# Keys and queries turned to feature layout by VectorE in 32x32 blocks, into tiles that already exist

## The chip, the cores and the metric

The kernel runs on one core of a Trainium2 chip. TensorE (PE in the profile) multiplies, VectorE (DVE) and ScalarE (ACT) work elementwise, GpSimd (POOL) does small things beside them, and SyncE (SP) issues nearly all transfers. Each engine works through its own list of instructions in order and waits at semaphores for the others. The metric is the time on the device in microseconds (us): the median of three runs before is 2010.44 us (2010.2 to 2012.16).

## What is computed

One layer of a streaming encoder, for 256 frames of a new stream (prompt) and 8 running streams with 16 frames each (sample). Together these are 384 tokens, three tiles of 128. What matters here, cut from the reference:

```
h   = rmsnorm(x);  proj = h @ w_in        # columns: GLU in | q | k | v | forget | gate A | gate B
q   = rmsnorm(q, q_norm_g);  k = rmsnorm(k, k_norm_g)      # 8 heads of 128
prompt:  softmax(q k^T / sqrt(128) + bias, causal) v
sample:  the same over 128 old keys and values of each stream, and its own new frames
u   = glu_a * sigmoid(glu_b);  depthwise conv over 31 frames, layernorm, swish, pointwise
x   = x + (sigmoid(gA) * conv_branch + sigmoid(gB) * attention) @ w_out
x   = x + gated FFN with a short convolution
```

Keys, values and forget logarithms of the new frames are outputs too.

## The kernel before

**Products.** Each float32 weight is split in two float32r parts, `hi` (a rounded copy, ScalarE, L145) and `lo` (the rest, VectorE, L146), and the activations likewise, so each product is three matmuls: hi·hi, hi·lo, lo·hi. `gemm` (L219 on) works on *blocks* of two k-tiles of weights (256 rows by 512 columns; a job of 16 k-steps takes 8 blocks). Three tags have three buffers each: `raw` (the block as loaded), `hi` and `lo`. A block's `hi` can be made only when TensorE has done with the block three places earlier, since that one's buffer is taken. So in steady state a `hi` starts when TensorE ends block n-3, and TensorE needs the split block after two more blocks.

**Order.** TensorE's list stands in program order (`manual_schedule` for that engine, L289). The lists of VectorE, ScalarE and SyncE are made by a scheduler from priorities; the splits (`ahead`, L197) and the evacuations have a raised priority. Once built, each list is fixed.

**The stages around the change.** The projection jobs run in this order: v (three jobs), k (two), q (two), GLU (four jobs of kind "A", where the weights are stationary and the 384 tokens stream by, L237 to L239), then the gates. k and q lie in `kt` and `qt`, tokens on the partitions. After the k jobs VectorE norms the keys (L517, L518) and after the q jobs the queries (L526), in the background of the next jobs.

**Attention** is done by steps hung on the k-steps of the four GLU jobs: after each k-step `tick` runs one step of `attention()` and one of `conv()`. A dictionary says at which tick a step of which head comes: `ATT_FIRST + 6 * head + offset`. The steps of one head are: `head_past_keys` (old keys turned by VectorE, L569), `head_operands` (three transposes of the queries and three of the new keys on TensorE into PSUM, L581 and L585, brought back by ScalarE as `qT` with a scale, L582, and by VectorE as `kT`, L586; then VectorE copies the sample queries into a zero-padded tile `qz`, L587), `head_scores` (products L593 to L601, the last eight of them with `qz`; then the softmax), `head_probs`, `head_out` and `head_last` (which write the head's rows of `attT`). `misc` PSUM tiles (three) serve all of these.

**Block transposes.** `blocks` (L253) already exists for the later stages: sixteen VectorE instructions at L257 turn three token tiles by 512 columns into feature layout. Each takes one group of 32 partitions, 12 blocks of 32x32.

Of the kernel before, what the change touches and what calls it, by code (L numbers as in the profile page):

```python
# [8 lines left out]
F32 = mybir.dt.float32  # L9
F32R = mybir.dt.float32r  # L10
AF = mybir.ActivationFunctionType
# [4 lines left out]
P = 128  # L16
DM = 2048
NT = 384
NTT = 3
H = 8  # L20
# [5 lines left out]

O_A, O_B, O_Q, O_K, O_V, O_GA, O_GB = 0, 1024, 2048, 3072, 4096, 5128, 7176

ATT_FIRST = 5
CONV_FIRST, CONV_LAG = 24, 17  # L30
LN_LAG = 18
SQ_LAG = 1
# [8 lines left out]
def hybrid_step(  # L41
# [9 lines left out]
    nc = tc.nc  # L51

    def pool(name, side="left", bufs=1, space=None):
        kw = dict(name=name, bufs=bufs, reuse_waits="tile")
        if space is not None:
            kw["space"] = space
        else:
            kw["side"] = side
        cm = tc.tile_pool(**kw)
        p = cm.__enter__()  # L60
        return p, lambda: cm.__exit__(None, None, None)
# [11 lines left out]
    def misc_tile():  # L73
        return misc.tile([P, 512], F32, tag="misc", name="misc")
# [4 lines left out]
    mm = nc.tensor.matmul  # L79
    tr = nc.tensor.transpose  # L80
# [26 lines left out]
    ident = cp.tile([P, P], F32, name="ident")  # L107
# [145 lines left out]
    def blocks(rows, put):  # L253
        src = rows.rearrange("p t (m b j) -> p b m t j", m=4, b=4)
        for b in range(4):
            for a in range(4):
                nc.vector.transpose(put(a, slice(32 * b, 32 * b + 32)), src[32 * a:32 * a + 32, b])  # L257

    def by_feature(dst):
        return lambda a, js: dst[js].rearrange("p m (t a i) -> p m t a i", t=NTT, a=4)[:, :, :, a]  # L260
# [75 lines left out]
    attT = p_t.tile([P, H, NT], F32, tag="T", name="attT")  # L336
# [3 lines left out]
    kt = p_qkv.tile([P, NTT, 1024], F32, name="kt")  # L340
    qt = p_qkv.tile([P, NTT, 1024], F32, name="qt")
# [36 lines left out]
    qgs = cp.tile([P, 1], F32, name="qgs")  # L378
# [136 lines left out]
    for t in range(NTT):  # L515
        k3 = kt[:, t, :].rearrange("p (h d) -> p h d", h=H)
        tt(k3, k3, rk[:, t, :].unsqueeze(2).to_broadcast([P, H, P]), op=ALU.mult)  # L517
        tt(k3, k3, kg[:].unsqueeze(1).to_broadcast([P, H, P]), op=ALU.mult)  # L518
    nc.sync.dma_start(prompt_k[0, 0].rearrange("(t p) h d -> p t (h d)", p=P), kt[:, 0:2, :])
    nc.sync.dma_start(sample_k[0].rearrange("b t h d -> (b t) (h d)"), kt[:, 2, :])  # L520

# [2 lines left out]
    for t in range(NTT):  # L524
        q3 = qt[:, t, :].rearrange("p (h d) -> p h d", h=H)
        tt(q3, q3, rq[:, t, :].unsqueeze(2).to_broadcast([P, H, P]), op=ALU.mult)  # L526


    p_att, close_att = pool("att", side="right")
    qz = [p_att.tile([P, 4, 2, 48], F32, name=f"qz{i}") for i in range(2)]  # L530
# [4 lines left out]
    def by_stream(ap):  # L535
        return ap.rearrange("p (g r t) -> p g r t", g=4, r=2)

    def padded(t_, b):
        r = b % 2
        return t_[:, b // 2].rearrange("p r x -> p (r x)")[:, 32 * r:32 * r + 32]  # L540
# [3 lines left out]
    def load_k(h):  # L544
        kc = kcs[h] = p_att.tile([P, 8 * P], F32, tag="kc", bufs=2, name="kc")
        for a in range(4):
            q = slice(32 * a, 32 * a + 32)
            nc.sync.dma_start(kc[q, :].rearrange("k (b j d) -> k b j d", b=8, j=4),
                              cache_k[0, :, :, h, q].rearrange("b (j k) d -> k b j d", j=4))

    def load_v(h):
        vc = p_att.tile([P, 8, P], F32, tag="vc", bufs=2, name="vc")
        nc.sync.dma_start(vc[:], cache_v[0, :, :, h, :].rearrange("b p d -> p b d"))
        bs = p_att.tile([P, 5 * P], F32, tag="bs", bufs=2, name="bs")
        nc.sync.dma_start(bs[:, 0:P], c_dr[h, 0:P].partition_broadcast(P))
        nc.sync.dma_start(bs[:, P:3 * P], c_dr[h, 0:2 * P].partition_broadcast(P))
        nc.sync.dma_start(bs[:, 4 * P:5 * P], c_dr[h, 2 * P:3 * P].partition_broadcast(P))
        nc.sync.dma_start(bs[:, 3 * P:4 * P], d_dr[:].rearrange("(b h) k -> b h k", h=H)[:, h:h + 1, :]
                          .to_broadcast([8, 16, P]))
        bc = bs[:, :4 * P].rearrange("p (a x) -> p a x", x=2 * P)[:, :, :P]  # L560
        nc.gpsimd.tensor_tensor(bc, bc, mk[:, 0:1, :].to_broadcast([P, 2, P]), op=ALU.add)
        nc.gpsimd.tensor_tensor(bs[:, 4 * P:], bs[:, 4 * P:], mk[:, 1, :], op=ALU.add)
        vbs[h] = vc, bs
# [3 lines left out]
    def head_past_keys(d):  # L567
        kTs = p_att.tile([P, 8, P], F32, tag="kTs", bufs=1, name="kTs")
        nc.vector.transpose(kTs[:].rearrange("p b k -> p (b k)"), kcs[d["h"]][:])  # L569
        d["kTs"] = kTs  # L570
        if d["h"] + 1 < H:
            load_k(d["h"] + 1)

    def head_operands(d):
        hs = d["hs"]
        d["vc"], d["bs"] = vbs[d["h"]]
        qT = p_att.tile([P, NT], F32, tag="qT", bufs=2, name="qT")
        kT = p_att.tile([P, NT], F32, tag="kT", bufs=2, name="kT")
        ps = misc_tile()
        for t in range(NTT):  # L580
            tr(ps[:, t * P:(t + 1) * P], qt[:, t, hs], ident[:])  # L581
        nc.scalar.activation(qT[:], ps[:, :NT], AF.Identity, scale=qgs[:])  # L582
        ps = misc_tile()
        for t in range(NTT):
            tr(ps[:, t * P:(t + 1) * P], kt[:, t, hs], ident[:])  # L585
        nc.vector.tensor_copy(kT[:], ps[:, :NT])  # L586
        nc.vector.tensor_copy(qz[d["h"] % 2][:, :, :, 0:16], by_stream(qT[:, 2 * P:]))  # L587
        d["qT"], d["kT"] = qT, kT

    def head_scores(d):  # L590
        qT, kT, kTs, bs, qzh = d["qT"], d["kT"], d["kTs"], d["bs"], qz[d["h"] % 2]
        s0 = misc_tile()
        mm(s0[:, :P], qT[:, 0:P], kT[:, 0:P], start=True, stop=True)  # L593
        s1 = misc_tile()
        mm(s1[:, :2 * P], qT[:, P:2 * P], kT[:, 0:2 * P], start=True, stop=True)  # L595
        s2_ = misc_tile()
        mm(s2_[:, P:2 * P], qT[:, 2 * P:], kT[:, 2 * P:], start=True, stop=True)
        for r in range(2):
            for g in range(4):
                b = 2 * g + r  # L600
                mm(s2_[32 * g:32 * g + 32, :P], padded(qzh, b), kTs[:, b, :], start=r == 0, stop=r == 1)  # L601
        pr = p_att.tile([P, 5 * P], F32, tag="pr", bufs=2, name="pr")
        mx = p_att.tile([P, 9], F32, tag="mx", bufs=2, name="mx")
        segs = [(s0, 0, 1), (s1, 1, 2), (s2_, 3, 2)]
        for i, (sp_, o, n) in enumerate(segs):
            v = pr[:, o * P:(o + n) * P]
            nc.vector.tensor_tensor_reduce(out=v, in0=sp_[:, :n * P], in1=bs[:, o * P:(o + n) * P], scale=1.0,
                                           scalar=-3.0e38, op0=ALU.add, op1=ALU.max, accum_out=mx[:, i:i + 1])
            ts(mx[:, 3 + i:4 + i], mx[:, i:i + 1], -1.0, None, op0=ALU.mult)
            nc.scalar.activation(v, v, AF.Exp, bias=mx[:, 3 + i:4 + i], accum_out=mx[:, 6 + i:7 + i])  # L610
            nc.vector.reciprocal(mx[:, i:i + 1], mx[:, 6 + i:7 + i])
            nc.scalar.activation(v, v, AF.Identity, scale=mx[:, i:i + 1])
        d["pr"] = pr
# [35 lines left out]
    def attention():  # L649
        at = {}  # L650
        for d in heads:
            for off, step in ((0, head_past_keys), (2, head_operands), (4, head_scores), (9, head_probs),
                              (11, head_out), (13, head_last)):
                at[ATT_FIRST + 6 * d["h"] + off] = step, d
        for t in range(max(at) + 1):
            if t in at:
                step, d = at[t]
                step(d)
                if step is head_out and d["h"] + 2 < H:
                    load_v(d["h"] + 2)  # L660
            yield
# [78 lines left out]
    load_v(0)  # L740
    load_v(1)
    att_steps = attention()
    gemm([job("A", 16, ha, glu_evac(g)) for g in range(4)], [att_steps, conv_steps])
    drain(att_steps)
# [175 lines left out]
    for u, i0 in enumerate(range(0, 11, 3)):  # L920
        n = min(3, 11 - i0)
# [141 lines left out]
```

## Time and profile before

| | |
|---|---|
| median of three runs | 2010.44 us |
| the profiled execution | 2010.56 us |
| its span, first to last instruction | 2008.6 us |
| TensorE busy | 1998.5 us, 99% |
| VectorE busy | 1242.1 us, 62% |
| ScalarE busy | 741.6 us, 37% |

The profiled execution is the one the rows are from; 2.0 us of its time lie outside the span. Busy shares are means over the whole span. A timeline row gives the start, the duration, the engine, the line and operation, what it writes and reads, how many instructions were merged, and in brackets how long the engine was idle before and for whom it waited. Matmuls overlap: the duration of one is longer than the distance to the next, so their pace is read from the starts.

### The profile page before, as it was taken

Reading aid. Unit: us, or ns where it says so; the run is one execution under the profiler, and the core shown is the slowest. Engines: PE = TensorE matmul, PEld = TensorE weight load, DVE = VectorE, ACT = ScalarE, POOL = GpSimd, SP = SyncE. Lnnn points to the kernel's source line nnn. Section 1 sums busy time; section 2 is a strip of 40 time slices with the busy share of each in tenths; the row PEclk is TensorE's granted clock in tenths of the full one; section 3 lists DMA queues with packets and bytes.
Section 4 is the critical chain, followed back from the end, with each engine's and each line's share of the span. In section 5 each row is a group of like instructions: output and inputs, shape, how many; then the busy total and the mean of one; then the engine's idle time right before and its main releaser. Section 6 shows DMA issues by size and latency. Waiting matters only on the chain.

```text
span 2008.6 us, 24550 instructions
## 1 busy us (share of the span) xinstructions
PE 1998.5 (99%) x9494; PEld 1686.6 (84%) x9494; DVE 1242.1 (62%) x1806; ACT 741.6 (37%) x1083; POOL 84.6 (4%) x214
## 2 busy tenths in 40 slices
PE   9999999999999999999999999999999999999999
PEld 8988999988888888888888888888888888888887
DVE  4434478888762645576767684367673376638663
ACT  5434454433333523334333432233332233323321
POOL 1000011100000000000000010000000000000000
PEclk9999999999999999999999999999999999999999
DMA  6566466344433353334343434434443434343443
GB/s 185 171 175 176 138 158 170 121 135 131 140 126 126 131 183 120 134 121 132 121 137 126 137 117 136 133 124 125 133 137 126 127 126 136 127 126 126 137 155 107
DMA packets 200574, 275.99 MB, mean 137 GB/s; under 512 B 45022, under 2 KB 88049, under 8 KB 200449
## 3 DMA queue, kind: packets, MB, share of 16 engines
q1 hardware_dynamic: 200137, 273.85, 43.5%
q8 instruction: 74, 1.21, 0.2%
q0 software_dynamic: 288, 0.57, 0.1%
q14 instruction: 43, 0.35, 0.1%
q10 hardware_dynamic: 32, 0.01, 0.0%
HBM read 266.98 MB, written 7.86 MB: 137 GB/s over the span
## 4 chain that ended last, share of the span: by engine, by line
PE 98%; DVE 1%; DMA 1%; ACT 0%; issue 0%; SPq 0%; ACTq 0%
PE acc L242 29%; PE acc L244 29%; PE acc L243 29%; PE acc L237 2%; PE acc L239 2%; PE acc L238 2%; DMA raw<-in_w_in_dram 1%; DVE uT L257 0%; DVE lo L146 0%; PE misc L845 0%; PE misc L634 0%; PE misc L601 0%; PE misc L283 0%; PE misc L620 0%; PE misc L595 0%
## 5 line engine op out<-in xcount | busy, mean ns | idle before, releaser
L146 DVE TENSOR_TENSOR lo<-raw,hi 128x1024 fp32r<-128x1024 f32 (+2 forms) x481 | 579.0, 1204 | 624.0 <-ACT hi L145 621.5
L145 ACT CAST hi<-raw 128x1024 fp32r<-128x1024 f32 (+2 forms) x481 | 496.0, 1032 | 1016.5 <-PE acc L244 900.3
L242 PE MATMUL acc<-hi,xg 128*128 128x512 f32 x1056 | 412.3, 390 | 0.0
L244 PE MATMUL acc<-hi,xg 128*128 128x512 f32 x1056 | 411.0, 389 | 0.0
L243 PE MATMUL acc<-lo,xg 128*128 128x512 f32 x1056 | 410.8, 389 | 0.0
L242 PE MATMUL acc<-hi,hT 128*128 128x512 f32 (+1 forms) x704 | 267.6, 380 | 2.0 <-ACT hT L286 2.0
L244 PE MATMUL acc<-hi,hT 128*128 128x512 f32 (+1 forms) x704 | 265.4, 377 | 0.4 <-DVE hT L287 0.4
L243 PE MATMUL acc<-lo,hT 128*128 128x512 f32 (+1 forms) x704 | 265.1, 377 | 0.0
L242 PEld LDWEIGHTS acc<-hi,xg 128*128 128x128 f32 x1056 | 198.2, 188 | 42.1
L244 PEld LDWEIGHTS acc<-hi,xg 128*128 128x128 f32 x1056 | 198.2, 188 | 41.3
L243 PEld LDWEIGHTS acc<-lo,xg 128*128 128x128 f32 x1056 | 198.3, 188 | 40.8
L242 PE MATMUL acc<-hi,act 128*128 128x512 f32 x528 | 205.5, 389 | 0.5 <-DVE y L1008 0.5
L243 PE MATMUL acc<-lo,act 128*128 128x512 f32 x528 | 205.4, 389 | 0.0
L244 PE MATMUL acc<-hi,act 128*128 128x512 f32 x528 | 205.4, 389 | 0.0
L720 DVE SCALAR_TENSOR_TENSOR ut<-ext,cw,ut 128x384 f32<-128x384 f32 x240 | 151.9, 633 | 6.2
L242 PEld LDWEIGHTS acc<-hi,hT 128*128 128x128 f32 x704 | 132.4, 188 | 24.6 <-ACT hT L286 2.3
L244 PEld LDWEIGHTS acc<-hi,hT 128*128 128x128 f32 x704 | 132.4, 188 | 23.1 <-DVE hT L287 0.7
L243 PEld LDWEIGHTS acc<-lo,hT 128*128 128x128 f32 x704 | 132.5, 188 | 22.2
L257 DVE STREAM_TRANSPOSE extf<-tok 32x384 f32<-32x384 f32 x176 | 100.3, 570 | 30.9 <-ACT tok L944 28.2
L257 DVE STREAM_TRANSPOSE uT<-tok 32x384 f32<-32x384 f32 x176 | 100.3, 570 | 29.7 <-ACT tok L944 26.9
L242 PEld LDWEIGHTS acc<-hi,act 128*128 128x128 f32 x528 | 99.1, 188 | 21.3 <-DVE y L1008 0.9
L244 PEld LDWEIGHTS acc<-hi,act 128*128 128x128 f32 x528 | 99.1, 188 | 20.7
(287 smaller groups left out, 2068.4 us busy)
## 6 DMA issues: line engine op xcount, KB each, us to landing
raw<-in_w_up_dram SPq DMA_DIRECT2D x176, 512.0 KB, 3.4
raw<-in_w_in_dram SPq DMA_DIRECT2D x96, 512.0 KB, 3.3
raw<-in_w_down_dram SPq DMA_DIRECT2D x88, 512.0 KB, 3.4
raw<-in_w_in_dram SPq DMA_DIRECT2D x64, 256.0 KB, 2.9
raw<-in_w_out_dram SPq DMA_DIRECT2D x32, 512.0 KB, 3.4
raw<-in_w_att_out_dram SPq DMA_DIRECT2D x16, 512.0 KB, 3.5
raw<-in_conv_pw_out_dram SPq DMA_DIRECT2D x16, 512.0 KB, 4.4
raw<-in_w_in_dram SPq DMA_DIRECT2D x23, 344.0 KB, 3.3
```

The costliest lines, as they stand in the source:

```text
L145: nc.scalar.copy(hi[:, k, :o], raw[:, k, :o])
L146: tt(lo[:, k, :o], raw[:, k, :o], f(hi[:, k, :o]), op=ALU.subtract)
L237: mm(o, hi[:, kk, s], ah, start=st, stop=False)
L238: mm(o, hi[:, kk, s], al, start=False, stop=False)
L239: mm(o, lo[:, kk, s], ah, start=False, stop=sp)
L242: mm(o, ah[:, s], hi[:, kk, :n], start=st, stop=False)
L243: mm(o, ah[:, s], lo[:, kk, :n], start=False, stop=False)
L244: mm(o, al[:, s], hi[:, kk, :n], start=False, stop=sp)
L257: nc.vector.transpose(put(a, slice(32 * b, 32 * b + 32)), src[32 * a:32 * a + 32, b])
L720: stt(o, v, wc, o, op0=ALU.mult, op1=ALU.add)
```

## The change

After the keys are normed, `blocks` turns them on VectorE, 32 instructions for the eight heads, into `attT`: the tile in which the attention output is put later, head by head, after that head's keys have been read. After the queries are normed, 32 more turn these into `kt`, whose token-layout keys are no longer needed; ScalarE scales them there in place, one instruction per head (L533). The per-head tiles `qT` and `kT`, the six TensorE transposes per head and the two instructions that brought them back are gone. `head_past_keys` is called by `head_operands`, at the same tick; `ATT_FIRST` goes from 5 to 8, with the other offsets kept, so scores and all later steps of a head come three ticks later (tick 12 instead of 9 for the first head).

```diff
-ATT_FIRST = 5
+ATT_FIRST = 8
...
         tt(k3, k3, kg[:].unsqueeze(1).to_broadcast([P, H, P]), op=ALU.mult)
+    for n in range(2):
+        blocks(kt[:, :, 512 * n:512 * (n + 1)], by_feature(attT[:, 4 * n:4 * n + 4]))
...
         tt(q3, q3, rq[:, t, :].unsqueeze(2).to_broadcast([P, H, P]), op=ALU.mult)
+    qT = kt[:].rearrange("p t n -> p (t n)").rearrange("p (h x) -> p h x", h=H)
+    for n in range(2):
+        blocks(qt[:, :, 512 * n:512 * (n + 1)], by_feature(qT[:, 4 * n:4 * n + 4]))
+        for h in range(4 * n, 4 * n + 4):
+            nc.scalar.activation(qT[:, h], qT[:, h], AF.Identity, scale=qgs[:])
...
     def head_operands(d):
-        hs = d["hs"]
+        head_past_keys(d)
         d["vc"], d["bs"] = vbs[d["h"]]
-        qT = p_att.tile([P, NT], F32, tag="qT", bufs=2, name="qT")
-        kT = p_att.tile([P, NT], F32, tag="kT", bufs=2, name="kT")
-        ps = misc_tile()
-        for t in range(NTT):
-            tr(ps[:, t * P:(t + 1) * P], qt[:, t, hs], ident[:])
-        nc.scalar.activation(qT[:], ps[:, :NT], AF.Identity, scale=qgs[:])
-        ps = misc_tile()
-        for t in range(NTT):
-            tr(ps[:, t * P:(t + 1) * P], kt[:, t, hs], ident[:])
-        nc.vector.tensor_copy(kT[:], ps[:, :NT])
-        nc.vector.tensor_copy(qz[d["h"] % 2][:, :, :, 0:16], by_stream(qT[:, 2 * P:]))
-        d["qT"], d["kT"] = qT, kT
+        nc.vector.tensor_copy(qz[d["h"] % 2][:, :, :, 0:16], by_stream(qT[:, d["h"], 2 * P:]))
...
-            for off, step in ((0, head_past_keys), (2, head_operands), (4, head_scores), (9, head_probs),
+            for off, step in ((0, head_operands), (4, head_scores), (9, head_probs),
```

The scheduler lays the new instructions among the others, so the diff does not say where they stand. The first place is VectorE's list during the two q jobs, from the end of the norm of the keys. Before, it holds four `lo` of weight blocks, the evacuation of the first q job (L424) and the next `lo`; these blocks are the last two of the first q job and the first three of the second:

```order
L146 TENSOR_TENSOR lo_1559<-raw_1556,hi_1558 128x1024
L146 TENSOR_TENSOR lo_1583<-raw_1580,hi_1582 128x1024
L146 TENSOR_TENSOR lo_1607<-raw_1604,hi_1606 128x1024
L146 TENSOR_TENSOR lo_1631<-raw_1628,hi_1630 128x1024
L424 TENSOR_SCALAR qt_159<-acc_1458,rs1_145 128x512
L146 TENSOR_TENSOR lo_1685<-raw_1682,hi_1684 128x1024
```

The same place of the changed kernel, with the same five blocks under new numbers (1591, 1615, 1639, 1663, 1717):

```order
L257 STREAM_TRANSPOSE attT_150<-kt_158 32x12x32
L146 TENSOR_TENSOR lo_1591<-raw_1588,hi_1590 128x1024
L257 STREAM_TRANSPOSE attT_150<-kt_158 32x12x32 x6
L146 TENSOR_TENSOR lo_1615<-raw_1612,hi_1614 128x1024
L257 STREAM_TRANSPOSE attT_150<-kt_158 32x12x32 x6
L146 TENSOR_TENSOR lo_1639<-raw_1636,hi_1638 128x1024
L257 STREAM_TRANSPOSE attT_150<-kt_158 32x12x32 x7
L146 TENSOR_TENSOR lo_1663<-raw_1660,hi_1662 128x1024
L257 STREAM_TRANSPOSE attT_150<-kt_158 32x12x32 x2
L424 TENSOR_SCALAR qt_159<-acc_1490,rs1_145 128x512
L257 STREAM_TRANSPOSE attT_150<-kt_158 32x12x32 x9
L146 TENSOR_TENSOR lo_1717<-raw_1714,hi_1716 128x1024
```

Thirty-one transposes of keys now stand ahead of the third block's `lo` of the second q job, and 22 of them ahead of the evacuation L424.

The second place is VectorE's list at the start of the GLU jobs, from the last instruction of the norm of the queries to the first head's scores. Before, `lo` of GLU blocks 5 and 6 (counted from 0), the copy of the turned keys, `qz` of the first head and the first step of its softmax:

```order
L526 TENSOR_TENSOR qt_159<-qt_159,rq1r_1905 128x1024
L146 TENSOR_TENSOR lo_2059<-raw_2055,hi_2058 128x1024
L586 COPY kT_2087<-misc_2093 128x384
L146 TENSOR_TENSOR lo_2103<-raw_2099,hi_2102 128x1024
L587 COPY qz0_1918<-qT_2086 128x8x16
L607 ISA pr_2144,mx_2145<-misc_2130,bs_1935 128x128
```

The changed kernel there; the four `lo` are those of GLU blocks 5, 6, 7 and 8:

```order
L528 TENSOR_TENSOR qt_159<-qt_159,rq1r_1937 128x1024
L257 STREAM_TRANSPOSE kt_158<-qt_159 32x12x32 x3
L146 TENSOR_TENSOR lo_2124<-raw_2120,hi_2123 128x1024
L257 STREAM_TRANSPOSE kt_158<-qt_159 32x12x32 x10
L146 TENSOR_TENSOR lo_2155<-raw_2151,hi_2154 128x1024
L257 STREAM_TRANSPOSE kt_158<-qt_159 32x12x32 x19
L146 TENSOR_TENSOR lo_2194<-raw_2190,hi_2193 128x1024
L146 TENSOR_TENSOR lo_2225<-raw_2221,hi_2224 128x1024
L584 COPY qz0_1990<-kt_158 128x8x16
L603 ISA pr_2254,mx_2255<-misc_2240,bs_2007 128x128
```

All 32 transposes of queries, and the `lo` of four blocks, now stand between the norm of the queries and `qz` of the first head.

The third place is TensorE's list where the first head's scores come, in the changed kernel: the end of the first k-step of GLU block 6, the scores, and the second k-step's first matmul:

```order
L239 MATMUL acc_2026<-hT3_88,lo_2155 128x384
L589 MATMUL misc_2240<-attT_150,kt_158 128x128
L591 MATMUL misc_2242<-attT_150,kt_158 128x256
L593 MATMUL misc_2244<-attT_150,kt_158 128x128
L597 MATMUL misc_2244<-kTs_2170,qz0_1990 32x128 x8
L237 MATMUL acc_2023<-hT3_88,hi_2154 128x384
```

The eight products with `qz0_1990` stand ahead of the rest of block 6; before, the scores stood after the tenth k-step, at the end of block 4 (lo_2021), and now after the thirteenth.

## Rows read from the trace of the kernel before

**Rows 1.** The page: busy time of the engines, and the chain by engine.

```profile
PE 1998.5 (99%) x9494; PEld 1686.6 (84%) x9494; DVE 1242.1 (62%) x1806; ACT 741.6 (37%) x1083; POOL 84.6 (4%) x214
...
PE 98%; DVE 1%; DMA 1%; ACT 0%; issue 0%; SPq 0%; ACTq 0%
```

**Rows 2.** Waits of TensorE, longest first: for whom, us, times, longest.

```profile
PE misc L306 <- POOL ident masks.py:199: 2.5, 1, 2.5
...
PE misc L706 <- DVE pz L624: 0.3, 1, 0.3
```

**Rows 3.** TensorE's timeline, first head: its transposes, the matmul after, its scores.

```profile
233.64 0.49 PE L581 MATMUL misc<-ident,qt 128*128 128x128 f32 x3
...
234.47 0.33 PE L238 MATMUL acc<-hT,hi 128*128 128x384 f32 x1
...
238.48 0.38 PE L593 MATMUL misc<-kT,qT 128*128 128x128 f32 x2
...
239.45 0.64 PE L601 MATMUL misc<-kTs,qz 128*32 128x128 f32 x16
```

**Rows 4.** Groups by line and shape: count, busy us, mean ns of one.

```profile
L257 DVE STREAM_TRANSPOSE uT<-tok 32x384 f32<-32x384 f32 x176 | 100.3, 570 | 29.7 <-ACT tok L944 26.9
...
L569 DVE STREAM_TRANSPOSE kTs<-kc 128x1024 f32<-128x1024 f32 x8 | 9.9, 1239 | 0.0
...
L582 ACT ACTIVATE qT<-misc,qgs 128x384 f32<-128x384 f32 x8 | 4.6, 576 | 3.9 <-PE misc L581 3.9
...
L587 DVE COPY qz<-qT 128x128 f32<-128x128 f32 x8 | 2.3, 289 | 0.0
```

**Rows 5.** VectorE's timeline in a later stage: block transposes with a `lo` between.

```profile
1717.47 3.49 DVE L257 STREAM_TRANSPOSE uT<-tok 32x384 f32<-32x384 f32 x6
1720.99 1.23 DVE L146 TENSOR_TENSOR lo<-raw,hi 128x1024 fp32r<-128x1024 f32 x1
1722.25 1.16 DVE L257 STREAM_TRANSPOSE uT<-tok 32x384 f32<-32x384 f32 x2
```

**Rows 6.** VectorE's timeline in the q jobs.

```profile
168.18 1.22 DVE L518 TENSOR_TENSOR kt<-kt,kg 128x1024 f32<-128x1024 f32 x1
...
183.85 0.75 DVE L424 TENSOR_SCALAR qt<-acc,rs 128x512 f32<-128x512 f32 x1 [1.10 <-PE acc L244]
```

**Rows 7.** ScalarE's timeline in the q jobs.

```profile
185.08 0.29 ACT L431 ACTIVATE jk<-qt 128x128 f32<-128x128 f32 x1
...
186.82 1.04 ACT L145 CAST hi<-raw 128x1024 fp32r<-128x1024 f32 x1
```

**Rows 8.** TensorE's timeline: second q job, its third block, first GLU job.

```profile
184.33 0.39 PE L242 MATMUL acc<-hi,hT 128*128 128x512 f32 x1
...
192.72 0.39 PE L243 MATMUL acc<-lo,hT 128*128 128x512 f32 x1
...
216.97 0.33 PE L237 MATMUL acc<-hT,hi 128*128 128x384 f32 x1
```

**Rows 9.** VectorE's timeline at the start of the GLU jobs.

```profile
228.40 1.22 DVE L526 TENSOR_TENSOR qt<-qt,rq1r 128x1024 f32<-128x1024 f32 x1
```

**Rows 10.** TensorE's timeline near the start of the program.

```profile
7.92 0.49 PE L244 MATMUL acc<-hi,hT 128*128 128x344 f32 x1
8.20 0.49 PE L242 MATMUL acc<-hi,hT 128*128 128x344 f32 x1
...
16.35 0.43 PE L242 MATMUL acc<-hi,hT 128*128 128x344 f32 x1 [2.03 <-ACT hT L286]
...
17.56 0.32 PE L242 MATMUL acc<-hi,hT 128*128 128x344 f32 x1
17.72 0.32 PE L243 MATMUL acc<-lo,hT 128*128 128x344 f32 x1
```

**Rows 11.** Windows: PE, PEld, DVE, ACT, POOL busy us, then granted clock.

```profile
300.00:350.00 50.00, 49.73 (x381) 47.18 (x380) 43.57 (x103) 25.74 (x53) 5.87 (x9) 1.00 0.72 171
350.00:395.00 45.00, 45.00 (x303) 42.80 (x302) 37.96 (x67) 21.44 (x37) 6.54 (x10) 1.00 0.37 116
```

More of the change, by code (lines that the diff above doesn't have):

```diff
@@ L574, in head_operands @@
     def head_operands(d):
-        hs = d["hs"]
+        head_past_keys(d)
         d["vc"], d["bs"] = vbs[d["h"]]
-        qT = p_att.tile([P, NT], F32, tag="qT", bufs=2, name="qT")
-        kT = p_att.tile([P, NT], F32, tag="kT", bufs=2, name="kT")
-        ps = misc_tile()
-        for t in range(NTT):
-            tr(ps[:, t * P:(t + 1) * P], qt[:, t, hs], ident[:])
-        nc.scalar.activation(qT[:], ps[:, :NT], AF.Identity, scale=qgs[:])
-        ps = misc_tile()
-        for t in range(NTT):
-            tr(ps[:, t * P:(t + 1) * P], kt[:, t, hs], ident[:])
-        nc.vector.tensor_copy(kT[:], ps[:, :NT])
-        nc.vector.tensor_copy(qz[d["h"] % 2][:, :, :, 0:16], by_stream(qT[:, 2 * P:]))
-        d["qT"], d["kT"] = qT, kT
+        nc.vector.tensor_copy(qz[d["h"] % 2][:, :, :, 0:16], by_stream(qT[:, d["h"], 2 * P:]))
     def head_scores(d):
-        qT, kT, kTs, bs, qzh = d["qT"], d["kT"], d["kTs"], d["bs"], qz[d["h"] % 2]
+        qh, kh, kTs, bs, qzh = qT[:, d["h"]], attT[:, d["h"]], d["kTs"], d["bs"], qz[d["h"] % 2]
         s0 = misc_tile()
-        mm(s0[:, :P], qT[:, 0:P], kT[:, 0:P], start=True, stop=True)
+        mm(s0[:, :P], qh[:, 0:P], kh[:, 0:P], start=True, stop=True)
         s1 = misc_tile()
-        mm(s1[:, :2 * P], qT[:, P:2 * P], kT[:, 0:2 * P], start=True, stop=True)
+        mm(s1[:, :2 * P], qh[:, P:2 * P], kh[:, 0:2 * P], start=True, stop=True)
         s2_ = misc_tile()
-        mm(s2_[:, P:2 * P], qT[:, 2 * P:], kT[:, 2 * P:], start=True, stop=True)
+        mm(s2_[:, P:2 * P], qh[:, 2 * P:], kh[:, 2 * P:], start=True, stop=True)
         for r in range(2):
```

## The prediction

> **What bounds the kernel now.** I read the page's busy times and its chain first. TensorE is busy for 99% of the span and makes up 98% of the chain that ended last [rows 1]: a microsecond of TensorE's list that goes is a microsecond won, and one that TensorE waits is one lost. Its waits come next: five groups, of which the longest is 2.5 us before its very first matmul, and the shortest, 0.3 us, the only one in the stages of the change [rows 2]. So each `lo` and each attention operand is there in time today, and the question is which of them will be late. For that I read the timelines of TensorE, VectorE and ScalarE from the norm of the keys to the first head's scores [rows 3, 6 to 9]. The attention and convolution stage itself has little air on VectorE: busy 43.57 of 50 and 37.96 of 45 us, with TensorE busy throughout [rows 11].
>
> **What goes: 5.3 us of TensorE.** Without the six transposes of a head, L237 would start where L581 does, at 233.64, and L238 0.17 us later (the distance of two such matmuls); L238 stands at 234.47 [rows 3]. That is 0.66 us per head and 5.3 us for eight. All of it is on the chain, and TensorE's list gets nothing in return. The copies back to SBUF go too, but ScalarE scales eight times as before (0.576 us each [rows 4]), and neither engine is the bound.
>
> **What comes: 64 block transposes on VectorE.** The same shape, 32x384, took 570 ns [rows 4], and six of them, up to the next instruction, 3.52 us: 0.585 us each; a `lo` among them takes 1.26 us to the next [rows 5]. Reading from `kt` or `qt` instead of `tok` changes only a stride. The other bound for the pace is the transpose of old keys, 1024 columns in 1239 ns [rows 4], which is 0.465 us for 384 columns. I take 0.585, the row with the same access pattern. 64 of them are 37.4 us, and they are hidden only as long as no `lo` and no operand behind them in VectorE's list is late. Twice one is.
>
> [...]
>
> **First wait: the keys, in the second q job.** The norm of the keys ends at 168.18 + 1.22 = 169.40 [rows 6]. From there VectorE's new list is 22 transposes and four `lo` up to the evacuation L424: 22 x 0.585 + 4 x 1.26 = 17.9, so L424 starts at 187.3 instead of 183.85 and ends at 188.05 with its 0.75 us [rows 6]. The four blocks are in time: each `lo` comes at most 7 transposes after the one before, 5.4 us with itself, and the last, done at 186.2, is wanted one block (4.08 us, [rows 8]) after 184.33, at 188.4. But two things now hang on the late evacuation. ScalarE's squares of that tile (first at 185.08) wait for it, and behind them in ScalarE's list stands the `hi` of the second job's third block, 1.74 us after that first square [rows 7]: it ends at 188.1 + 1.74 + 1.05 = 190.9, harmless. On VectorE nine more transposes stand ahead of that block's `lo`: 188.05 + 9 x 0.585 + 1.23 = 194.5. TensorE wants it at 192.72 [rows 8]. So it waits 1.9 us (with 0.1 for the handover). With the quicker pace, 0.105 us less for each of 31, there is no wait at all.
>
> **Second wait: the queries, at the first head's scores.** All later times shift by the first wait alike, so I leave it out here. The norm of the queries ends at 228.40 + 1.22 = 229.62 [rows 9]. Behind it: 32 transposes, 18.7 us; the `lo` of blocks 5 and 6 among them, 2.5; the `lo` of blocks 7 and 8 behind them, 2.4; then `qz`, some 0.25 [rows 4, 5]. That is 253.5. None of these four `lo` has to wait for its own `hi`: the latest, block 8's, may start when TensorE ends block 5, at 216.97 + 12 x 2.085 = 242.0, and stands on ScalarE behind four scalings, which can start after the sixteenth transpose (241.6) and take 2.3 us, so it ends at about 245.
>
> When does TensorE come for `qz`? A k-step is 2.085 us: ten of them and one head's transposes lie between 216.97 and 238.48 [rows 3, 8]. The scores now come after 13, at 244.07; their first three products take 0.97 us (238.48 to 239.45 [rows 3]), and at 245.05 the eight products with `qz` stop TensorE until 253.5. That is 8.5 us. The three ticks of later start give 6.25 us, and without them the wait would be longer by as much. Queued behind it is everything TensorE has, above all the rest of GLU block 6; block 7's `lo` (252.1) and block 8's (253.3) would have made TensorE wait too, but less. Behind `qz` on VectorE the first head's softmax starts late but has five ticks, 10 us, till its probabilities are wanted. Quicker pace: 32 x 0.105 less, 5.1 us.
>
> **Third term: TensorE's pace after standing still.** [...] At the start of the program, after 2.5 us without work, 344-column matmuls stood 0.28 us apart at 8 us, where they stand 0.16 apart at 17.6; but 2.03 us of waiting at 14 to 16.35 changed nothing [rows 10]. So the price of 8.5 us of standing still has these ends (a gain is excluded, the clock being at its upper level): nothing, as after the 2.03 us, or the start's, about half of the 6 us from the first matmul at 2.5 to past 8.2, some 3.0 us. A wait four times as long as the harmless one is nearer to the start; I take 2.0. The first wait, 1.9 us, is like the harmless one: nothing.
>
> [...]
>
> **Sum.** -5.3 + 1.9 + 8.5 + 2.0 = +7.1 us on the profiled execution's 2010.56 us, that is 2017.7; the median of the runs stands 0.1 us lower, so 2017.5 us, 0.35% slower. Transfers bring nothing: the weight blocks are fetched in the same order, and a `raw` tile freed late by VectorE is refilled while TensorE waits for the same VectorE.
>
> **Rivals.**
> - *The pause costs no pace.* For it: the 2.03 us that changed nothing. Against: this pause is four times that. 2010.44 + 5.1 = 2015.5 us.
> - *A third wait, on the late VectorE.* The longer run of work between two `lo` late in the GLU jobs, with the convolution's taps, has little slack (VectorE 87% busy in 300 to 350 [rows 11]), and attention now lies three ticks later against the convolution. Against: kT's copies are gone there, and TensorE has no more than one wait of 0.3 us there today. Half a block to a block, 2 to 4 us, comes on top: 2020.5 us.
> - *The cheap transposes.* VectorE turns the blocks at the pace of L569's row or better. Then the first wait is gone, the second is 5.1 us, and the gain of 5.3 us pays for it: 2010.2 us with no loss of pace, 2012 with it. It decides from about 0.49 us per transpose on, and at 0.4 us (second wait 2.6) the change is faster, by 2.7 us: 2007.7, or below 2006.4 with 0.36. For it: the row of L569. Against it: two groups of 32x384 that took 570 ns with just this pattern.
>
> **Chances and range.** A measurement of this kernel tells about 0.2%, 4 us, from no change: 2006.4 to 2014.5 is the same. Forecast 0.52, the pause that costs no pace 0.22, the third wait 0.14, cheap transposes 0.12. The first is slower whole, the second for 0.18 of its 0.22 (2015.5 lies 1 us above the bound), the third whole; cheap transposes split evenly. Slower 0.84, same 0.10, faster 0.06. The range takes in the second and the third rival and the inner end of the fourth: 2012.5 to 2021.
>
> **What would show it.** Right: PE waiting once for a `lo` (VectorE, L146) by about 2 us near 193, and once for `qz` (L584) by 8 to 9 us near 247, L257 at 0.57 to 0.59 us; L424 of the first q job at 187; 344- or 384-column matmuls at twice their spacing for a few us after the second wait; no other wait of TensorE above 1 us up to 400 us, and everything later shifted as a whole. Wrong: VectorE's transposes clearly below 0.5 us, `qz` there before 247, or waits of TensorE in the convolution stage.

## The result, and the profile after

The changed kernel takes 2019.0 us (2018.84 to 2020.17, five runs), the kernel before beside it 2010.8 us: a ratio of 1.0042 [1.0031, 1.0052], slower by 0.42%. The forecast was 2017.5 us, within 2012.5 to 2021.0. The profiled execution spans 2016.9 us, 8.3 more than before.

The page of the changed kernel, its busy times and its chain by engine:

```profile
PE 1996.8 (99%) x9446; PEld 1683.6 (83%) x9446; DVE 1275.6 (63%) x1862; ACT 740.9 (37%) x1083; POOL 88.2 (4%) x214
...
PE 93%; DVE 5%; issue 1%; ACT 1%; DMA 0%; SPq 0%; DVEq 0%; ACTq 0%
```

Beside [rows 1], TensorE has 48 instructions fewer, VectorE 56 more (64 block transposes come, eight copies go) and 33.5 us more work. TensorE's busy time hardly changes, yet 5% of the chain now runs over VectorE. Where, the waits of TensorE say (for whom, us, times, longest):

```profile
PE misc L597 <- DVE qz L584: 8.4, 1, 8.4
PE misc L306 <- POOL ident masks.py:199: 2.5, 1, 2.5
PE acc L243 <- DVE lo L146: 1.7, 1, 1.7
PE acc L242 <- ACT hT L286: 1.4, 1, 1.4
PE misc L626 <- DVE mx L603: 0.7, 1, 0.7
```

Against [rows 2] three are new: the two forecast, `lo` and `qz`, and a small one on `mx`; the one of 0.3 us on `pz` is gone. VectorE's timeline shows what stands ahead of the two operands, first in the second q job, then at the first head:

```profile
186.88 0.75 DVE L424 TENSOR_SCALAR qt<-acc,rs 128x512 f32<-128x512 f32 x1
187.66 5.25 DVE L257 STREAM_TRANSPOSE attT<-kt 32x384 f32<-32x384 f32 x9
192.94 1.22 DVE L146 TENSOR_TENSOR lo<-raw,hi 128x1024 fp32r<-128x1024 f32 x1
...
241.42 11.09 DVE L257 STREAM_TRANSPOSE kt<-qt 32x384 f32<-32x384 f32 x19
252.54 2.36 DVE L146 TENSOR_TENSOR lo<-raw,hi 128x1024 fp32r<-128x1024 f32 x2
254.82 0.22 DVE L584 COPY qz<-kt 128x128 f32<-128x128 f32 x1
```

VectorE has no gap here: nine transposes in 5.28 us up to the `lo`, nineteen in 11.12 up to the next, 0.585 us each both times. It is the length of the list ahead that makes both late, not something VectorE waits for. TensorE's timeline at the same two places:

```profile
194.22 0.50 PE L243 MATMUL acc<-lo,hT 128*128 128x512 f32 x1 [1.67 <-DVE lo L146]
...
255.09 1.08 PE L597 MATMUL misc<-kTs,qz 128*32 128x128 f32 x16 [8.38 <-DVE qz L584]
256.10 0.69 PE L237 MATMUL acc<-hT,hi 128*128 128x384 f32 x1
256.59 0.52 PE L238 MATMUL acc<-hT,hi 128*128 128x384 f32 x1
256.91 0.52 PE L239 MATMUL acc<-hT,lo 128*128 128x384 f32 x1
...
260.75 0.36 PE L239 MATMUL acc<-hT,lo 128*128 128x384 f32 x1
260.94 0.34 PE L237 MATMUL acc<-hT,hi 128*128 128x384 f32 x1
```

After the long wait the 384-column matmuls start 0.32 us apart, up to 260.75, and from there 0.17 to 0.19. The windows around it (PE, PEld, DVE, ACT, POOL busy us, then the granted clock, the DMA share, GB/s):

```profile
245.00:250.00 5.00, 1.71 (x11) 1.46 (x9) 4.89 (x9) 1.27 (x2) 0.00 (x0) 1.00 0.03 8
250.00:255.00 5.00, 0.00 (x0) 0.00 (x0) 4.92 (x9) 2.44 (x5) 0.00 (x0) 0.55 0.04 5
255.00:258.00 3.00, 2.91 (x22) 2.50 (x23) 2.50 (x14) 1.97 (x5) 0.00 (x0) 0.50 0.95 287
258.00:262.00 4.00, 4.00 (x18) 4.00 (x17) 1.30 (x5) 3.25 (x7) 0.17 (x1) 0.65 0.73 188
262.00:270.00 8.00, 8.00 (x49) 7.96 (x49) 4.12 (x8) 5.07 (x9) 4.43 (x6) 1.00 0.55 148
```

The granted clock fell while TensorE stood still: it reads 1.00 from 245 to 250 us, 0.55 from 250 to 255 and 0.50 from 255 to 258, and the matmuls are back at their distance of before some 5.7 us after TensorE went on (from 260.75). That cost 2.6 us: the products with `qz` and the gap behind them took 1.50 us (255.09 to 256.59) where 0.85 is their time at a clock of 1.00 (254.70 to 255.55 in the run `filler` below), and the 13 matmuls from 256.59 to 260.75 took 4.16 us instead of 13 x 0.173 = 2.25.

The first wait, of 1.67 us, left the clock at 1.00 (190 to 200 us).

The small wait is that of a later head, VectorE first, then TensorE:

```profile
353.96 3.28 DVE L716 SCALAR_TENSOR_TENSOR ut<-ext,cw,ut 128x384 f32<-128x384 f32 x3
357.16 2.62 DVE L146 TENSOR_TENSOR lo<-raw,hi 128x1024 fp32r<-128x1024 f32 x2
359.70 0.28 DVE L603 CUSTOM_DVE_ANT_0 pr<-misc,bs 128x128 f32<-128x128 f32 x1
```

```profile
360.04 0.49 PE L626 MATMUL misc<-vt,pT 128*128 128x128 f32 x2 [0.75 <-DVE mx L603]
```

Three convolution taps and two `lo`, 5.7 us, stand ahead of the masked scores, which must leave their PSUM tile before L626 may write there.

**Where the time went.** Two landmarks are the same work in each kernel: TensorE's first 384-column matmul (the first GLU job, at 216.97 in before [rows 8]) and its first gate matmul behind the last GLU job. The second one of before, then both of after:

```profile
389.62 0.39 PE L242 MATMUL acc<-hi,hT 128*128 128x512 f32 x1
...
218.60 0.33 PE L237 MATMUL acc<-hT,hi 128*128 128x384 f32 x1
397.87 0.48 PE L242 MATMUL acc<-hi,hT 128*128 128x512 f32 x1
```

So +1.6 us came ahead of the GLU jobs, +6.6 within them (179.27 instead of 172.65), and the span's +8.3 is reached before the gate starts; nothing more comes later. The +1.6 is a sum of two: from the first matmul of the second q job to the GLU jobs it takes 34.61 us instead of 32.64, so the wait of 1.67 us costs 2.0 (the runs below take 32.64 or 34.61 to 34.63, without and with it), and -0.3 comes from the start of the program, which the change does not touch.

### The profile page after: what moved, and what is told of

Its sections match the earlier page's. It is cut to its first block, busy times and chain, and to the rows that moved or that the text cites. A ratio compares the mean times of both kernels' runs of the same rounds, so it can differ in the third digit from the quotient of the medians.

```text
span 2016.9 us, 24500 instructions
## 1 busy us (share of the span) xinstructions
PE 1996.8 (99%) x9446; PEld 1683.6 (83%) x9446; DVE 1275.6 (63%) x1862; ACT 740.9 (37%) x1083; POOL 88.2 (4%) x214
## 4 chain that ended last, share of the span: by engine, by line
PE 93%; DVE 5%; issue 1%; ACT 1%; DMA 0%; SPq 0%; DVEq 0%; ACTq 0%
PE acc L242 29%; PE acc L244 29%; PE acc L243 28%; PE acc L237 2%; PE acc L238 2%; PE acc L239 2%; DVE lo L146 1%; DVE kt L257 1%; DVE attT L257 1%; DVE ut L716 1%; DMA raw<-in_w_in_dram 0%; DVE uT L257 0%; PE misc L841 0%; PE misc L630 0%; PE misc L597 0%
```

## Experiments

Theory: each loss is an instruction that stands behind block transposes in VectorE's list (once a `lo`, once `qz`), plus the clock's fall through the second wait; the saving on TensorE is real and stays. Rivals: VectorE transposes disturb what runs beside them wherever they are; the slow matmuls come from the burst of transfers behind the wait; the later start of attention is part of the loss. One figure serves all runs: the stretch between the two landmarks in the profiled execution, 172.65 us in before. A run's time is the median of its executions, with the ratio to before and its 95% interval; views and stretches are from the profiled execution.

**Does the clock fall because TensorE stands still?** `filler` gives TensorE matmuls to do in the `qz` wait of head 0, into an unused part of a PSUM tile.

```diff
         mm(s2_[:, P:2 * P], qh[:, 2 * P:], kh[:, 2 * P:], start=True, stop=True)
+        if d["h"] == 0:
+            for _ in range(36):
+                mm(s1[:, 2 * P:3 * P], ident[:], ident[:], start=True, stop=True)
```

> The changed kernel with 36 matmuls of ident by ident, 128x128, into an unused part of a PSUM tile, ahead of the first head's products with qz: work for TensorE inside its wait of 8.4 us. One such float32 product took about 0.22 us (the first product of the scores in the trace of before), so 36 take 7.9 us and fit in the wait. Theory (TensorE's lower pace after the wait comes from standing still): the granted clock stays 1.00, matmuls after the wait stand 0.17 us apart at once, and the time falls by some 2.5 us, from 2019.0 to about 2016.5. Rival (the matmuls after the wait are slow because the transfers held up by VectorE land all together there, 95% of the DMA engines' time in 255 to 258 us): the pace is as low as before and the time does not fall, 2019.

2017.37 us, ratio 1.0031 [1.0019, 1.0044]; stretch 176.72, which is 2.55 us less than after. TensorE's timeline (each float32 product counts as two instructions, so 36 are 72) and the windows behind it:

```profile
246.15 8.20 PE L596 MATMUL misc<-ident 128*128 128x128 f32 x72
254.70 0.65 PE L600 MATMUL misc<-kTs,qz 128*32 128x128 f32 x16 [0.34 <-DVE qz L584]
255.27 0.44 PE L237 MATMUL acc<-hT,hi 128*128 128x384 f32 x1
255.55 0.34 PE L238 MATMUL acc<-hT,hi 128*128 128x384 f32 x1
```

```profile
255.00:258.00 3.00, 3.00 (x31) 2.80 (x21) 1.90 (x8) 2.08 (x6) 0.00 (x0) 1.00 0.98 317
258.00:262.00 4.00, 4.00 (x25) 4.00 (x25) 2.67 (x8) 2.67 (x6) 0.17 (x1) 1.00 0.53 141
```

`qz` is as late as before, the burst of transfers is even denser (317 GB/s against 287), and the clock stays at 1.00. The burst is innocent; standing still cost 2.6 us on top of the wait. From 255 to 258 us the clock was 0.50 after 8.4 us of standing and 1.00 when the same time was filled.

**Does the later start matter?** `tick5` is the changed kernel with attention from tick 5, `start8_alone` the kernel before with attention from tick 8.

The edit of `tick5` (the other is its reverse):

```diff
-ATT_FIRST = 8
+ATT_FIRST = 5
```

> The changed kernel with ATT_FIRST back at 5: the first head's scores after 10 k-steps instead of 13. VectorE's list then has 32 transposes and three lo (not four) ahead of qz. Theory: qz ready at 229.6 + 32 x 0.585 + 3 x 1.26 + 0.2 = 252.3, wanted at 216.97 + 10 x 2.085 + 0.97 = 238.8: a wait of 13.5 us instead of 8.4, lower clock for as long as before: 2019.0 + 5.1, about 2024. Rival (the wait is made of something that moves with the steps, such as the old keys' transfer or the scores' PSUM tiles): the same 8 us, about 2019.

> The kernel before with one number changed: attention from tick 8 in place of 5. Theory (the later start costs and gains nothing, since all heads still end ahead of the last GLU tick): 2010.8, within 0.7, no wait of TensorE above 1 us that before hasn't. Rival (the later start is part of the loss or of the gain): 2 us or more away from before, with a wait on mx or on sgb that wasn't there.

`tick5`: 2023.63 us, ratio 1.0064 [1.005, 1.0077], with these waits:

```profile
PE misc L597 <- DVE qz L584: 10.1, 1, 10.1
PE misc L589 <- ACT kt L533: 3.0, 1, 3.0
```

TensorE comes three ticks, 6.25 us, earlier for a `qz` that, counted from the first GLU matmul, is only 1.3 us earlier (one `lo` less stands ahead of it), and waits longer: 13.1 us in two places, the first of them for ScalarE's scaling of the turned queries (L533). `start8_alone`: 2010.09 us, 0.9995 [0.9987, 1.0004], stretch 172.16, no new wait. The later start costs nothing by itself, and in the changed kernel it spares 4.7 us of waiting; of the stretch it spares 3.2 us (182.45 in `tick5`), since in `tick5` the wait on `mx` is missing and the clock comes back sooner (0.88 in 258 to 262 us, 0.65 in after). That the medians lie 4.6 apart is in part the start of the program, of which the last section tells: the GLU jobs of `tick5` begin at 220.14, 1.5 us later than in after.

**Each half alone.** `keys_only` is before with the keys turned by VectorE, attention from tick 5; `queries_only` is after with the keys left to TensorE.

On the kernel before, for `keys_only`:

```diff
+    for n in range(2):
+        blocks(kt[:, :, 512 * n:512 * (n + 1)], by_feature(attT[:, 4 * n:4 * n + 4]))
 ...
-        for t in range(NTT):
-            tr(ps[:, t * P:(t + 1) * P], kt[:, t, hs], ident[:])
-        nc.vector.tensor_copy(kT[:], ps[:, :NT])
```

On the changed kernel, for `queries_only`:

```diff
-    for n in range(2):
-        blocks(kt[:, :, 512 * n:512 * (n + 1)], by_feature(attT[:, 4 * n:4 * n + 4]))
-    qT = kt[:].rearrange("p t n -> p (t n)").rearrange("p (h x) -> p h x", h=H)
+    qT = attT
```

> The kernel before with the keys alone turned by VectorE (in the two blocks behind the normalization, as in after), queries still turned by TensorE per head, attention still from tick 5. Theory (each part has its own wait in VectorE's list): half of the TensorE saving, -2.4, and the lo wait of the second q job, +1.7, no qz wait; time 2010.8 - 0.7 = 2010.1 (2009.3 to 2011). Rival (the price lies in the attention reading tiles that VectorE wrote, or in the later start): a wait on qz or kT of several us, 2014 or more.

> The changed kernel with the queries alone turned by VectorE (into the tile of the attention output), keys turned by TensorE per head as before, attention from tick 8. Theory: half of the TensorE saving, -2.4, the qz wait of head 0, 8.1 to 8.4, the lower clock behind it, 2.6, perhaps 0.5 of the small wait on mx; no lo wait; time 2010.8 + 8.9 = 2019.7 (2018.5 to 2021). Rival (the two parts share one price, so that half the transposes pay half of it): about 2015.

The longest wait of each in the stages of the change, `keys_only` first:

```profile
PE acc L243 <- DVE lo L146: 1.7, 1, 1.7
```

```profile
PE misc L592 <- DVE qz L587: 9.3, 1, 9.3
```

`keys_only` takes 2009.58 us, 0.9994 [0.9985, 1.0003]: its stretch is 169.90, 2.75 shorter with the same small wait on `pz` in it as before, and it pays 2.0 ahead of it, for the wait of 1.7. `queries_only` takes 2020.2 us, 1.0041 [1.0029, 1.0054], stretch 181.19: no `lo` wait, all of the `qz` wait, the clock at 0.50 from 250 to 258. The wait is longer than the 8.1 to 8.4 forecast because TensorE stops already at the first product of the scores (L592): VectorE's copy of the head's keys (L586, 255.12 to 255.67) now stands behind the transposes too, right ahead of `qz`. The prices belong one to each half, as forecast, and the keys alone are no loss.

**Can both waits be avoided?** `later_queries` turns heads 4 to 7's queries from tick 10 of the GLU jobs, one block instruction in a tick. `paced_both` does that too, and also turns the keys in the second q job, four block instructions behind each `lo`.

```diff
-    for n in range(2):
-        blocks(qt[:, :, 512 * n:512 * (n + 1)], by_feature(qT[:, 4 * n:4 * n + 4]))
...
+    for _ in turn_queries(0):
+        pass
...
+    gemm([job("A", 16, ha, glu_evac(g)) for g in range(4)], [att_steps, conv_steps, later_queries()])
```

In `paced_both` moreover:

```diff
+    gemm([job("B", 16, ha, tok_evac(qt, 512 * i, 512, 1)) for i in range(2)], [key_steps])
```

> The changed kernel with the queries of heads 4 to 7 turned one block instruction per tick of the GLU jobs from the tenth on, instead of all at once after the norm; keys as in the changed kernel. VectorE's list then has 16 transposes and three lo ahead of the first head's qz. Theory (the loss is what stands ahead of qz in VectorE's list): qz ready at 229.6 + 16 x 0.585 + 3 x 1.26 + 0.2 = 243 us on the clock of before, wanted at 245: the wait of 8.4 us and the lower clock behind it go, the wait of 1.7 us for lo in the second q job stays: 2010.8 - 5.3 + 1.8, about 2007.3. Rival (33 us more of VectorE work cost this wherever it stands, since VectorE is 87% busy in the convolution stage): the same work comes later in that stage and TensorE waits there instead, 2015 or more.

> As later_queries, and the keys turned in the second q job, four block instructions behind each lo, held back by order alone. Theory: no wait of TensorE is left from the change and only the six transposes per head are missing: 2010.8 - 5.3 = 2005.5 us, TensorE waiting for nothing above 1 us after the first 30 us. Rival (the gain of 5.3 us is not on the path, or the convolution stage takes it back): 2009 or more.

`later_queries`: 2011.88 us, 1.0006 [0.9998, 1.0015]; `paced_both`: 2009.63 us, 0.9993 [0.9984, 1.0002]. Both lie above what I expected, by 4.6 and 4.1 us. By its number `paced_both` is even where its rival had put it (2009 or more). The forecast waits went (`qz` in both, `lo` in the second), but a new one came. TensorE in `later_queries`, then in `paced_both`, then VectorE in `paced_both`:

```profile
256.85 0.44 PE L238 MATMUL acc<-hT,hi 128*128 128x384 f32 x1 [2.88 <-DVE sgb L684]
```

```profile
256.76 0.44 PE L240 MATMUL acc<-hT,hi 128*128 128x384 f32 x1 [2.89 <-DVE sgb L698]
```

```profile
254.41 0.57 DVE L260 STREAM_TRANSPOSE kt<-qt 32x384 f32<-32x384 f32 x1
255.01 1.23 DVE L149 TENSOR_TENSOR lo<-raw,hi 128x1024 fp32r<-128x1024 f32 x1
256.16 1.01 DVE L698 TENSOR_TENSOR sgb<-acc,rs1b 128x384 f32<-128x384 f32 x2
```

The evacuation of the first GLU job (`sgb`, `ut`) now stands behind the deferred transposes, and the second job cannot get its PSUM tile. I had looked at the two consumers I knew and had pushed the work in front of a third. Beside these 2.9 us the net saving is smaller than the 5.3 I had counted on (4.8 by the table below), and some clock was lost, of which the last section tells.

**The third consumer, by itself.** `past_evac` is `paced_both` with the deferred transposes after that evacuation, two in a tick and each held behind the newest `lo`; so their place and their pace change together.

```diff
-Q_LATER = 10
+Q_LATER = 17
...
-        yield from block_steps(qt[:, :, 512 * n:512 * (n + 1)], by_feature(qT[:, 4 * n:4 * n + 4]))
+        steps = block_steps(qt[:, :, 512 * n:512 * (n + 1)], by_feature(qT[:, 4 * n:4 * n + 4]), n == 1)
+        for i, _ in enumerate(steps):
+            if i % 2:
+                yield
```

> As paced_both, but the query transposes of heads 4 to 7 start at tick 17 of the GLU (two in a tick, each behind the newest lo), after the evacuation of the first GLU job, and not at tick 10. Theory (the 2.9 us left in paced_both are the first GLU job's evacuation, sgb, standing behind deferred transposes in VectorE's list; nothing else is lost): that wait goes, no other comes, the stretch from the first GLU matmul to the first gate matmul is 4.6 to 4.8 us shorter than in before (172.65 us there), so about 168 us; time 2006.5 (2005 to 2007.5). Rival (the transposes slow what runs beside them, or wait somewhere else, wherever they are put): a new wait of 2 to 3 us in a later tick, time 2009 to 2010.

2007.03 us (2005.13 to 2007.86), ratio 0.9979 [0.997, 0.9988]. VectorE at the evacuation, and TensorE's longest wait in the stages of the change:

```profile
251.33 1.23 DVE L149 TENSOR_TENSOR lo<-raw,hi 128x1024 fp32r<-128x1024 f32 x1 [1.15 <-ACT hi L148]
...
252.55 1.00 DVE L701 TENSOR_TENSOR sgb<-acc,rs1b 128x384 f32<-128x384 f32 x2
```

```profile
PE misc L659 <- DVE mx L636: 0.7, 1, 0.7
```

The evacuation starts 3.6 us earlier, its wait is gone, the one on `mx` I had not expected, and the stretch is 168.26, 4.39 us shorter than before. With the same 64 transposes on the same VectorE the longest wait of TensorE left in these stages is this one of 0.74 us: the rival by which they disturb wherever they stand has fallen. This version beats both kernels.

## Why the prediction was right

| term | forecast | measured |
|---|---|---|
| six transposes of a head, eight times, net | -5.3 | -4.8 |
| first wait, `lo` in the second q job | +1.9 | +2.0 (1.67 of waiting) |
| second wait, `qz` of the first head | +8.5 | +8.4 |
| pace after standing still | +2.0 | +2.6 |
| small wait on `mx`, less the 0.3 on `pz` of before | none | +0.5 |
| start of the program | none | -0.3 |
| sum | +7.1 | +8.3 (the span; the rounded terms give 8.4) |

The mechanism came out as forecast: two consumers behind the transposes in VectorE's list, each late by the length of that list, and a lower clock (0.50) behind the long wait. No large errors cancel. That the sum is 1.2 us low comes from the saving, the clock and the small wait, each some 0.5 us worse than forecast.

- *What goes.* The stretch grew by 6.62; its waits grew by 8.38 + 0.75 - 0.27, the clock took 2.56, so 4.80 were saved. `past_evac` gives the same without the clock: 4.39 + 0.74 - 0.27 = 4.86. `paced_both` gives 1.94 + 2.89 - 0.27 = 4.56. So a head saves 0.57 to 0.61 us net. The 0.66 read off the first head's timeline [rows 3] was no misreading: the last head of before gives the same (L581 at 352.94, L238 at 353.77, 0.17 between two such matmuls). What I had wrong is that TensorE's list gets nothing in return. In `past_evac` the scores of three later heads take 0.46 us more in all, in waits too short for the list of TensorE's waits. Most of it is in head 5, where the third product starts 0.68 us after the second and not 0.43 as in head 4, behind VectorE's copy of the head before. TensorE in head 4, TensorE in head 5, VectorE in head 5:

```profile
310.57 0.60 PE L624 MATMUL misc<-attT,kt 128*128 128x256 f32 x2
311.00 0.38 PE L626 MATMUL misc<-attT,kt 128*128 128x128 f32 x2
...
327.56 0.60 PE L624 MATMUL misc<-attT,kt 128*128 128x256 f32 x2
328.24 0.49 PE L626 MATMUL misc<-attT,kt 128*128 128x128 f32 x2
...
327.90 0.28 DVE L653 COPY pz<-misc 128x128 f32<-128x128 f32 x1
```

- *Pace of the transposes.* 570 ns each and 0.585 from one to the next, as in [rows 4, 5] for the same pattern; reading from `kt` or `qt` changed nothing. The rival of cheap transposes, for which the 1024-column row spoke, is out.
- *First wait.* L424 was at 186.88 (forecast 187.3), the `lo` done at 194.16 (194.5) and TensorE going on 0.06 us later (0.1), 1.67 us of waiting (1.9).
- *Second wait.* `qz` came at 255.0 and TensorE for it at 246.7, both later than forecast (253.5 and 245.05) by some 1.6, the shift ahead of the GLU jobs, which I had left out on both sides: 8.38 against 8.5.
- *Pace.* The rival without a price is out: 2.6 us, within the bounds of 0 and 3.0, and nearer to the start's 3.0 than to the 2.0 that I took. That bound was weaker than it looked: the granted clock of before reads 1.00 from 6 to 10 us too, where those matmuls stood 0.28 us apart, so no row shows that they were slow for the clock. The price itself rests on `filler`. A gain was excluded with the clock of before: it reads 1.00 in [rows 11], and no window of these runs reads more.
- *A third wait.* There was one, but of 0.7 us, not half a block; it is in `past_evac` too, at the same taps.

The change as made is 0.42% slower than before; `past_evac`, with the same 37 us of transposes in other places of VectorE's list, is 0.21% faster. Here it was the place in the list that decided.

## What to carry to other kernels

Moving work from the bounding engine to an idle one pays only if nothing that the bounding engine needs stands behind that work in the idle engine's list. Go through that list for every consumer, not just the operands of the moved work: here three cost more than a microsecond (`lo`, `qz` and the evacuation of a PSUM tile), and I found the last one only by running into it. The pause of 8.4 us cost TensorE 2.6 us more than its length, so read the clock behind a pause.

## What the runs showed of the hardware

After waits of 2 to 3 us the clock fell in some executions and not in others. The `sgb` wait of 2.9 us, on the same matmul of the same job, left the granted clock at 0.57 from 258 to 262 in `later_queries` and at 1.00 in `paced_both`:

```profile
258.00:262.00 4.00, 4.00 (x16) 4.00 (x15) 3.87 (x8) 2.12 (x5) 1.96 (x4) 0.57 0.54 144
```

```profile
258.00:262.00 4.00, 4.00 (x27) 3.96 (x26) 3.87 (x8) 3.48 (x7) 1.88 (x4) 1.00 0.53 140
```

The stretches differ by 1.6 us (172.32 and 170.71), which is about what this clock takes. The same happens at the start of the program, which no kernel here changes. There TensorE waits for `hT`, 0.3 to 3.1 us in the ten profiles; before waited 2.03 us and kept its clock [rows 10], `start8_alone` waited 2.12 us and did not. Before, then `start8_alone`:

```profile
16.00:20.00 4.00, 3.28 (x20) 2.98 (x21) 2.56 (x4) 3.49 (x9) 0.00 (x0) 1.00 0.81 255
```

```profile
16.00:20.00 4.00, 3.62 (x14) 3.34 (x14) 2.01 (x4) 2.94 (x8) 0.00 (x0) 0.61 0.83 250
```

At the start the ten profiles part by the length of this wait: after the five of 0.3 to 2.03 us the clock of 16 to 20 us reads 1.00, after the five of 2.12 to 3.1 us 0.58 to 0.68. The wait of 2.03 us, by which I priced the pause in part, is the longest of those that kept the clock. By length alone the two `sgb` waits cannot be told apart, so what decides is open; no run here tells.

The price at the start can be read from the end of the wait to the same matmul some 20 us later: 19.87 us in before (16.35 to 36.22), 21.46 in `start8_alone` (15.80 to 37.26). So a comparison of two single profiles is uncertain by some 1.6 us for this alone, and by the differing wait on top: the profile of `past_evac` has no `lo` wait, yet its GLU jobs begin at 218.47, 1.5 us later than in before, since its start waited 2.5 us and went on at 0.68. The runs of one kernel scatter by as much (of the six of `filler`, two took 2015.5 to 2015.7 and four 2017.4). The stretches between the two landmarks leave the start out.
